# A mask that moves from TensorE into each head's bias on GpSimd, and three changed orders

## The chip, the cores and the metric

The kernel runs on one core of a Trainium2 chip. The metric is device time in microseconds (us) of one execution, as the median of the runs. PE is TensorE, DVE is VectorE, ACT is ScalarE, POOL is GpSimd, and SP is SyncE, which issues nearly all DMAs here.

## The reference, cut to what matters

Two decoder layers over 512 positions of 1024 channels, in float32. Layer 0 mixes by stick-breaking attention, layer 1 by an indexer-selected attention; each is followed by a gated MLP with a causal convolution of width 3. The second attention, for 16 heads:

```python
isc = jnp.where(causal[None], isc, NEG)          # indexer scores
_, sel = lax.top_k(isc, topk)                    # 128 keys for each query
valid = sel <= t[None, :, None]
logits = jnp.einsum('bqhd,bqkd->bqhk', qb, kg) * scale
bias = rel_bias[t5_bucket(t[None, :, None] - sel)]   # by distance, per head
logits = logits + bias
logits = jnp.where(valid[:, :, None, :], logits, NEG)
p = jax.nn.softmax(logits, axis=-1)
o = jnp.einsum('bqhk,bqkd->bqhd', p, vg)         # then w_uv, w_out
```

The kernel doesn't gather. It takes all keys up to the query's block and adds a mask of 0 or -1e30, the same for all heads, so that exactly the selected keys are left.

## The kernel before, in words

**Layout and precision.** Activations lie channel-first, 8 tiles of 128 channels by 512 positions. A product of full precision is three matmuls on a high and a low part (`mm3`, L248 to L250): high by high, low by high, high by low. A weight chunk is 128 x 1024. SP fetches it into one of six `raw` tiles (L177); `split_hi` (L208) rounds it on ACT into `whi`; `split_lo` (L216) subtracts on DVE, or on an engine it is given, into `wlo`. `whi` and `wlo` have four buffers each. All chunks follow one list, `order`; `chunk(key, 0)` returns a chunk and splits it on the spot if that hasn't happened.

**Order.** The whole kernel is under a manual schedule: each engine, and SP's queue of DMA issues, runs its instructions in the order in which the code emits them. What an instruction waits for holds up all behind it on that engine.

**Stages.** First attention (to about 245 us), its last output quarter together with the norm of the next sub-layer (`boundary`), the first feed-forward layer (to 620), `boundary`, projections and the indexer (to 770), the second attention (to 911), `boundary`, the second feed-forward layer, and the output.

**`boundary` (L376)** projects the last four chunks (`last`) in two halves of 256 positions, eight tiles each (`out_steps`, tile `pt_l`, two PSUM buffers under the tag "tr"). After each tile DVE adds it to the residual (`add_to_x`, L359) and ACT squares it. It starts by calling `chunk(k, 0)` for all four chunks.

**`bias_rows` (L167)** computes, for 16 heads and 640 distances, the bias table: two matmuls of 320 columns (L171, tile `pt_b`, tag "x", which has one buffer), each copied out by DVE (L172), and a DMA to DRAM on SP (L173). It is called before up-step 4 of the first feed-forward layer, `bias_load` before step 3. An up-step is two output tiles of 24 matmuls of 512 columns, then convolution, gate and split on ACT and DVE.

**The second attention (from L1270).** `load_bias` (L1313) fetches a head's bias as a 128 x 512 tile `th` (two buffers) whose columns run backwards. `logits(h, j)` makes query block j against its (j+1)*128 keys: three matmuls and a fourth of the identity by the mask in bf16 (L1334), which adds the mask in PSUM (tile `z`, two buffers). `softmax` scales and adds the bias (DVE, L1342) into one tile `L` per head (two buffers) and takes the row maximum (L1344); `expo` is ACT (L1349). `transposed(h, pi)` turns the block columns in three pieces on PE (L1360) and copies them out on ACT or DVE. `weighted` multiplies a pair of heads by its values (`av`), `pair_values` makes these (`pv`, tag "x"), `pair_scale` turns the reciprocal sums (`bc`, tag "x"), and `pair_hi`, `pair_lo` make the high and low parts of the pair's output `O`.

In iteration h the loop works on the transposes of head h and the logits and softmax of head h+1. Between them `fill(n)` emits n steps of other PE work, three matmuls of 512 columns each: the projections of queries 12 to 15, then the first half of the output projection (`do` chunks, tile `pt_o`), 60 steps in all. `LATE_STEPS[h]` steps go to head h, half in the middle, half at the end. Behind each step one pending event is emitted, such as splitting the next chunk or adding a finished tile.

Of the kernel before, what the change touches and what calls it, by code (L numbers as in the profile page):

```python
# [18 lines left out]
D = 1024  # L19
S = 512  # L20
# [17 lines left out]
EARLY_Q = 12  # L38
LATE_STEPS = [2, 3, 2, 3, 3, 3, 3, 3, 3, 3, 5, 5, 5, 5, 5, 8]
AHEAD = 2  # L40
# [78 lines left out]
def kernel_body(ctx, tc, xT, wst, cst, smalls, crow, ccol, relb, onehot, outT):  # L119
# [46 lines left out]

    def bias_rows():  # L167
        rsb = raws.tile([P, D], F32, name="rsb", tag="raw")[:HEADS, :640]
        for c in range(2):
            pt = ptile([P, S], "pt_b", "x")  # L170
            pe.matmul(pt[:HEADS, :320], lhsT=rel, rhs=bias["oh"][:, c * 320:(c + 1) * 320], start=True, stop=True)  # L171
            dve.tensor_copy(rsb[:, c * 320:(c + 1) * 320], pt[:HEADS, :320])  # L172
        nc.sync.dma_start(rb, rsb)  # L173

# [201 lines left out]
    def boundary(last, O, l, gate, nxt, first):  # L376


        cks = [chunk(k, 0) for k in last]
        nl, gcol, sh, sc = nxt  # L380
# [27 lines left out]
        for m in range(KT):  # L408
            t = out_tile(0, m)
            if prev is not None:  # L410
                square_add(m - 1, prev)
            prev = t
            if m == 4:
                warm(AF.Abs_reciprocal_sqrt)
# [547 lines left out]
    def ffn_layer(l, first, man):  # L962
        with ExitStack() as st:
# [54 lines left out]
            for step, i in ffn_steps():  # L1018
                if step == "up" and i < 2:
                    continue  # L1020
                if l == 0 and step == "up" and i in (3, 4):
                    (bias_load if i == 3 else bias_rows)()
                if step == "up":
                    up(i)
                elif step == "down":
                    down(i)
# [10 lines left out]
    def dsa_layer(l, first, man):  # L1037
        with ExitStack() as st:
# [233 lines left out]
            with ExitStack() as sa:  # L1272
# [9 lines left out]
                def late_steps():  # L1282

                    g, pt = late, late_pt
                    for h in range(EARLY_Q, HEADS):
                        if h > EARLY_Q:
                            pt = ptile([P, S], "pt_q", "mm")
                            g = project_steps(pt, chunk(("dq", h), 0))
                        for _ in g:
                            yield  # L1290
                        events.extend([lambda h=h, pt=pt: q_hi(h, pt), lambda h=h, pt=pt: (q_lo(h, pt), split_hi()),
                                       lambda h=h: (split_lo(), q_sum(h))])
                    events.append(lambda: q_norm(EARLY_Q, HEADS))
# [19 lines left out]
                def load_bias(h):  # L1313
                    th = ths[h] = ap.tile([P, S], F32, name="th", bufs=2)
                    ov = rb[h:h + 1, 0:1]
                    nc.sync.dma_start(th, bass.AP(tensor=ov.tensor, offset=ov.offset, ap=[[1, P], [1, S]]))

                def begin(h):
                    L = ap.tile([P, LW], F32, name="L")
# [3 lines left out]
                    heads[h] = (L, ap.tile([P, QT], F32, name="nm"), ap.tile([P, QT], F32, name="sum"), heads["rv"], {})  # L1323

                def logits(h, j):
                    qh, ql = Q[h]
                    ns = (j + 1) * P
                    qs = slice(j * P, ns)
                    ls = slice(LOFF[j], LOFF[j] + ns)
                    z = heads[h][4][j] = ptile([P, S], "z", "z")  # L1330
                    pe.matmul(z[:, :ns], lhsT=qh[:, qs], rhs=kph[:, :ns], start=True, stop=False)
                    pe.matmul(z[:, :ns], lhsT=ql[:, qs], rhs=kph[:, :ns], start=False, stop=False)
                    pe.matmul(z[:, :ns], lhsT=qh[:, qs], rhs=kpl[:, :ns], start=False, stop=False)
                    pe.matmul(z[:, :ns], lhsT=ident_b, rhs=maskb[:, ls], start=False, stop=True)  # L1334

                def softmax(h, j):
                    L, nm, sum_, rv, z = heads[h]
                    z = z.pop(j)
                    ns = (j + 1) * P
                    ls = slice(LOFF[j], LOFF[j] + ns)  # L1340
# [3 lines left out]
                    dve.tensor_reduce(nm[:, j:j + 1], L[:, ls], axis=AX.X, op=OP.max, negate=True)  # L1344

                def expo(h, j):
                    L, nm, sum_ = heads[h][:3]
                    ls = slice(LOFF[j], LOFF[j] + (j + 1) * P)
                    act.activation(L[:, ls], L[:, ls], AF.Exp, bias=nm[:, j:j + 1], accum_out=sum_[:, j:j + 1])  # L1349

                trs = {}

                def transposed(h, pi, by_act):
                    L = heads[h][0]
                    tr = ptile([P, S], "tr", "tr")
                    w = TRW[pi]
                    for i, c0 in TRP[pi]:
                        for j in range(i, QT):
                            c = c0 + (j - i) * P
                            pe.transpose(tr[:, c:c + P], L[:, LOFF[j] + i * P:LOFF[j] + (i + 1) * P], ident)  # L1360
                    if pi == 0:
# [4 lines left out]
                    else:  # L1366
                        dve.tensor_copy(t, tr[:, :w])

                vals = {}
# [61 lines left out]
                def sums(h):  # L1431

                    dve.reciprocal(heads[h][3][:, :, h % 2], heads[h][2])
                    return pair_sums(heads[h][3]) if h % 2 else None

                for h in range(HEADS):
# [165 lines left out]
```

## Time and profile before

| | us |
|---|---|
| median of 3 runs | 1310.35 (1310.23 to 1310.48) |
| the profiled execution | 1311.1 |
| its span, first to last instruction | 1309.0 |
| busy PE, DVE, ACT, POOL | 1283.9, 930.9, 591.8, 35.9 |

Busy times are unions of the spans of an engine's instructions. Matmuls overlap one another, so PE's share of 98% doesn't say that it works at its peak; a wait of PE shows best as the step from the start of one matmul to the start of the next. A bracket behind an instruction tells how long its engine sat idle before it, and what ended that.

### The profile page before, as it was taken

The numbers are of one execution on the slowest core, as the hardware profiler recorded it, in microseconds if no ns is written. First come the engines' busy times: TensorE is split into PE (matmuls) and PEld (weight loads), VectorE is DVE, ScalarE is ACT, GpSimd is POOL, SyncE is SP. The second block draws the span as 40 slices with busy tenths as digits, with TensorE's granted clock in tenths as the row PEclk, the third lists the DMA queues.
The fourth block names the chain that finished last, engine by engine and source line by source line (L and its number), as shares of the span: only waits on it lengthen the run. The fifth ranks groups of instructions, "written<-read, shape, count | busy, mean of one in ns | idle before, by whom it ended". The sixth has DMA issues, their size and how long they took to land.

```text
span 1309.0 us, 17994 instructions
## 1 busy us (share of the span) xinstructions
PE 1283.9 (98%) x6979; PEld 1069.9 (82%) x6988; DVE 930.9 (71%) x1532; ACT 591.8 (45%) x1049; POOL 35.9 (3%) x27
## 2 busy tenths in 40 slices
PE   8999999998999999999999999999999999999998
PEld 6978787896888888888987777776998888888888
DVE  5888889688677877885778877777776546546653
ACT  5576666464333433443555446565554334334430
POOL 0000000000000000000102320000000000000000
PEclk9999999999999999999999999999999999999999
DMA  9644444322576575654222301213222432433221
GB/s 374 203 129 129 145 129 133 109 69 80 210 242 192 177 243 191 194 174 153 76 65 81 97 26 54 66 58 121 79 83 73 121 97 73 121 97 97 73 89 65
DMA packets 50613, 163.23 MB, mean 125 GB/s; under 512 B 5808, under 2 KB 8624, under 8 KB 50528
## 3 DMA queue, kind: packets, MB, share of 16 engines
q1 hardware_dynamic: 50096, 161.30, 38.4%
q8 instruction: 55, 0.90, 0.3%
q10 hardware_dynamic: 432, 0.79, 0.2%
q14 instruction: 30, 0.25, 0.1%
HBM read 159.92 MB, written 2.14 MB: 124 GB/s over the span
## 4 chain that ended last, share of the span: by engine, by line
PE 91%; DVE 4%; ACT 2%; DMA 1%; issue 1%; SPq 0%; another core or an unknown queue 0%; DVEq 0%; ACTq 0%
PE pt_u L248 11%; PE pt_u L250 11%; PE pt_u L249 11%; PE pt_d L250 5%; PE pt_d L249 5%; PE pt_d L248 5%; PE pt_first L249 2%; PE pt_first L248 2%; PE pt_first L250 2%; PE pt_l L248 2%; PE pt_q L248 2%; PE pt_l L250 2%; PE pt_l L249 2%; PE pt_q L250 2%; PE pt_q L249 2%; PE pt_qk L248 2%
## 5 line engine op out<-in xcount | busy, mean ns | idle before, releaser
L208 ACT ACTIVATE whi<-raw 128x1024 fp32r<-128x1024 f32 (+1 forms) x206 | 205.1, 1002 | 122.1 <-PE pt_d L250 95.5
L248 PE MATMUL pt_u<-hhi,whi 128*128 128x512 f32 x640 | 250.1, 391 | 0.0
L249 PE MATMUL pt_u<-hhi,wlo 128*128 128x512 f32 x640 | 249.8, 390 | 0.0
L250 PE MATMUL pt_u<-hlo,whi 128*128 128x512 f32 x640 | 249.7, 390 | 0.0
L216 DVE TENSOR_TENSOR wlo<-raw,whi 128x1024 fp32r<-128x1024 f32 (+1 forms) x194 | 223.5, 1154 | 17.8 <-ACT whi L208 16.9
L973 ACT ACTIVATE y<-pt_u,sm 128x512 f32<-128x512 f32 x80 | 62.2, 777 | 200.3 <-PE pt_u L250 200.3
L248 PEld LDWEIGHTS pt_u<-hhi,whi 128*128 128x128 f32 x640 | 120.7, 189 | 26.1 <-issue 1.0
L249 PEld LDWEIGHTS pt_u<-hhi,wlo 128*128 128x128 f32 x640 | 120.7, 189 | 25.1
L250 PEld LDWEIGHTS pt_u<-hlo,whi 128*128 128x128 f32 x640 | 120.7, 189 | 25.1
L974 DVE SCALAR_TENSOR_TENSOR y<-pt_u,sm,y 128x511 f32<-128x511 f32 x80 | 59.9, 749 | 105.9 <-ACT y L973 105.9
L248 PE MATMUL pt_d<-acthi,whi 128*128 128x512 f32 x288 | 112.0, 389 | 0.0
L249 PE MATMUL pt_d<-acthi,wlo 128*128 128x512 f32 x288 | 112.0, 389 | 0.0
L250 PE MATMUL pt_d<-actlo,whi 128*128 128x512 f32 x288 | 112.0, 389 | 0.0
L257 DVE SCALAR_TENSOR_TENSOR raw<-raw,cond 128x1024 f32<-128x1024 f32 x88 | 106.5, 1216 | 1.1 <-DMA raw<-wst 1.1
L359 DVE SCALAR_TENSOR_TENSOR x<-pt_d,mod,x 128x512 f32<-128x512 f32 x48 | 36.0, 749 | 72.8 <-PE pt_d L250 72.8
L232 ACT ACTIVATE acthi<-y 128x512 fp32r<-128x512 f32 x44 | 27.8, 632 | 104.3 <-DVE y L992 104.3
L248 PE MATMUL pt_first<-hhi,whi 128*128 128x256 f32 (+1 forms) x224 | 68.6, 306 | 0.3 <-ACT whi L208 0.3
L249 PE MATMUL pt_first<-hhi,wlo 128*128 128x256 f32 (+1 forms) x224 | 67.1, 300 | 0.9 <-DVE wlo L216 0.8
L250 PE MATMUL pt_first<-hlo,whi 128*128 128x256 f32 (+1 forms) x224 | 66.9, 299 | 0.0
L249 PEld LDWEIGHTS pt_d<-acthi,wlo 128*128 128x128 f32 x288 | 54.1, 188 | 11.3
L248 PEld LDWEIGHTS pt_d<-acthi,whi 128*128 128x128 f32 x288 | 54.1, 188 | 11.2
L250 PEld LDWEIGHTS pt_d<-actlo,whi 128*128 128x128 f32 x288 | 54.1, 188 | 11.2
(253 smaller groups left out, 2662.4 us busy)
## 6 DMA issues: line engine op xcount, KB each, us to landing
raw<-wst SPq DMA_DIRECT2D x250, 512.0 KB, 3.7
raw<-wst SPq DMA_DIRECT2D x48, 384.0 KB, 3.0
th<-rb SPq DMA_DIRECT2D x16, 256.0 KB, 3.7
ada<-wst SPq DMA_DIRECT2D x4, 512.0 KB, 6.2
outT<-x SPq DMA_DIRECT2D x16, 128.0 KB, 1.7
x<-xT SPq DMA_DIRECT2D x5, 256.0 KB, 4.9
x<-xT ACTq DMA_DIRECT2D x3, 256.0 KB, 3.9
cond<-crow SPq DMA_DIRECT2D x1, 512.0 KB, 10.7
```

Source lines behind the costliest of these rows:

```text
L208: act.activation(hi[:, :n], raw[:, :n], AF.Copy)
L216: engine.tensor_sub(lo[:, :n], raw[:, :n], hi[:, :n].bitcast(F32))
L232: act.activation(hi, src, AF.Copy)
L248: pe.matmul(out, lhsT=whi, rhs=ahi, start=start, stop=False)
L249: pe.matmul(out, lhsT=wlo, rhs=ahi, start=False, stop=False)
L250: pe.matmul(out, lhsT=whi, rhs=alo, start=False, stop=stop)
L257: dve.scalar_tensor_tensor(raw, raw, 1.0, cond, op0=OP.mult, op1=OP.mult, accum_out=dst)
L359: dve.scalar_tensor_tensor(x[f][:, c], pt, mod[l][:, g * KT + f:g * KT + f + 1], x[f][:, c], op0=OP.mult, op1=OP.add)
L973: act.activation(y, pt, AF.Identity, scale=cw[2], bias=sm[:, b + S_CB + c:b + S_CB + c + 1])
L974: dve.scalar_tensor_tensor(y[:, 1:], pt[:, :S - 1], cw[1], y[:, 1:], op0=OP.mult, op1=OP.add)
```

## The change

The mask matmul goes. Each head's bias gets the mask added on GpSimd before it is used: `masked_bias(h, j)` writes `Ls[h, j]`, a tile of its own per query block (two buffers each), from the reversed bias tile and the mask. Heads 0 and 1 get theirs at the start; head h+2 gets block 0 behind the first transposes of head h, block 1 behind the second, blocks 2 and 3 behind the third. `softmax` then scales the logits and adds in place. Bias tiles are fetched two heads further ahead. Low parts of the eight chunks split in this stage go to GpSimd. The three orders: `bias_rows` does its halves before up-steps 4 and 5; `boundary` splits what is left of its last two chunks between the tiles of its first half; in the last head `pair_values` comes ahead of the filler. `LATE_STEPS` has other numbers.

```diff
-LATE_STEPS = [2, 3, 2, 3, 3, 3, 3, 3, 3, 3, 5, 5, 5, 5, 5, 8]
+LATE_STEPS = [3, 3, 3, 3, 3, 3, 3, 3, 3, 4, 5, 5, 5, 5, 4, 6]
...
+    def bias_rows(c):
+        if c == 0:
+            bias["rows"] = raws.tile([P, D], F32, name="rsb", tag="raw")[:HEADS, :640]
+        pt = ptile([P, S], "pt_b", "x")
+        pe.matmul(pt[:HEADS, :320], lhsT=rel, rhs=bias["oh"][:, c * 320:(c + 1) * 320], start=True, stop=True)
+        dve.tensor_copy(bias["rows"][:, c * 320:(c + 1) * 320], pt[:HEADS, :320])
+        if c:
+            nc.sync.dma_start(rb, bias["rows"])
...
-        cks = [chunk(k, 0) for k in last]
+        cks = [chunk(k, 0) for k in last[:2]]
+        unsplit = lambda: pos["i"] <= order.index(last[3])
...
+            if m in (0, 3) and unsplit():
+                split_hi()
+            if m in (1, 4):
+                split_lo()
+                if m == 4:
+                    while unsplit():
+                        split_hi()
+                        split_lo()
+            if m in (3, 5):
+                cks.append(chunk(last[len(cks)], 0))
...
-                if l == 0 and step == "up" and i in (3, 4):
-                    (bias_load if i == 3 else bias_rows)()
+                if l == 0 and step == "up" and 3 <= i < 6:
+                    bias_load() if i == 3 else bias_rows(i - 4)
...
-                                       lambda h=h: (split_lo(), q_sum(h))])
+                                       lambda h=h: (split_lo(engine=pool), q_sum(h))])
...
-                        events.extend([split_hi, split_lo])
+                        events.extend([split_hi, lambda: split_lo(engine=pool)])
...
+                def masked_bias(h, j):
+
+                    ns = (j + 1) * P
+                    Ls[h, j] = ap.tile([P, ns], F32, name=f"L{j}")
+                    pool.tensor_add(Ls[h, j], ths[h][:, :ns][:, ::-1], maskb[:, LOFF[j]:LOFF[j] + ns])
...
-                    pe.matmul(z[:, :ns], lhsT=qh[:, qs], rhs=kpl[:, :ns], start=False, stop=False)
-                    pe.matmul(z[:, :ns], lhsT=ident_b, rhs=maskb[:, ls], start=False, stop=True)
+                    pe.matmul(z[:, :ns], lhsT=qh[:, qs], rhs=kpl[:, :ns], start=False, stop=True)
...
-                    dve.scalar_tensor_tensor(L[:, ls], z[:, :ns], rq[:, c:c + 1], ths[h][:, :ns][:, ::-1],
-                                             op0=OP.mult, op1=OP.add)
+                    dve.scalar_tensor_tensor(L, z[:, :ns], rq[:, c:c + 1], L, op0=OP.mult, op1=OP.add)
...
+                    if h + 2 < HEADS:
+                        for j in ((0,), (1,), (2, 3))[pi]:
+                            masked_bias(h + 2, j)
...
                 load_bias(0)
                 load_bias(1)
+                for h in range(2):
+                    for j in range(QT):
+                        masked_bias(h, j)
+                    load_bias(h + 2)
...
                     if not more:
                         rvb = sums(h)
+                        pair_values(h - 1)
...
-                    if h % 2:
+                    if h % 2 and more:
                         pair_values(h - 1)
...
-                        if n + 1 < HEADS:
-                            load_bias(n + 1)
+                        if n + 3 < HEADS:
+                            load_bias(n + 3)
```

## Rows read from the trace of the kernel before

**Rows 1.** The page: its span, the ended-last chain by engine, one group of DMA issues.

```profile
span 1309.0 us, 17994 instructions
...
PE 91%; DVE 4%; ACT 2%; DMA 1%; issue 1%; SPq 0%; another core or an unknown queue 0%; DVEq 0%; ACTq 0%
...
raw<-wst SPq DMA_DIRECT2D x250, 512.0 KB, 3.7
```

**Rows 2.** Windows by stage: stretch, length, busy us per engine (instructions), clock, DMA.

```profile
770.00:914.00 144.00, 138.72 (x872) 107.55 (x880) 104.94 (x213) 83.67 (x221) 0.00 (x0) 1.00 0.23 72
```

**Rows 3.** PE's timeline: the 512-column mask matmul and its successor.

```profile
782.56 0.39 PE L1334 MATMUL z<-maskb,ident_b 128*128 128x512 bf16 x1
...
782.79 0.38 PE L1360 MATMUL tr<-cons,L 128*128 128x128 f32 x2
```

**Rows 4.** PE's timeline at the bias rows: start, us, instruction, idle before it.

```profile
318.75 0.71 PE L171 MATMUL pt_b<-oh,rel 32*16 32x320 f32 x2
324.78 1.24 PE L171 MATMUL pt_b<-oh,rel 32*16 32x320 f32 x2 [5.32 <-DVE rsb L172]
325.95 0.79 PE L248 MATMUL pt_u<-hhi,whi 128*128 128x512 f32 x1
...
330.74 0.39 PE L250 MATMUL pt_u<-hlo,whi 128*128 128x512 f32 x1
```

**Rows 5.** Windows of 4 us behind the bias rows and the last seam.

```profile
324.00:328.00 4.00, 3.22 (x7) 1.79 (x8) 2.33 (x4) 0.56 (x1) 0.00 (x0) 0.50 0.05 11
...
918.00:922.00 4.00, 4.00 (x23) 4.00 (x23) 1.09 (x3) 0.42 (x1) 0.00 (x0) 0.61 0.43 154
```

**Rows 6.** DVE's and SP's timelines at the bias rows.

```profile
324.25 0.47 DVE L172 COPY rsb<-pt_b 16x320 f32<-16x320 f32 x1
...
326.56 0.33 SPq L173 DMA_DIRECT2D rb<-rsb  x1
326.95 32.89 SPq L177 DMA_DIRECT2D raw<-wst  x15
```

**Rows 7.** DVE's and PE's timelines at the seams of 914 and 622.

```profile
913.98 2.36 DVE L216 TENSOR_TENSOR wlo<-raw,whi 128x1024 fp32r<-128x1024 f32 x2 [0.26 <-ACT whi L208]
...
917.07 0.38 PE L248 MATMUL pt_l<-ohi,whi 128*128 128x256 f32 x1 [2.55 <-DVE x L359]
...
626.05 0.36 PE L248 MATMUL pt_l<-acthi,whi 128*128 128x256 f32 x1 [1.00 <-DVE x L359]
```

**Rows 8.** POOL's timeline: copies at 650, a low part beside the top-k.

```profile
649.66 0.76 POOL L1148 COPY work<-cons 128x128 f32<-128x128 f32 x1
...
650.62 1.78 POOL L1148 COPY work<-cons 128x128 f32<-128x128 f32 x1
...
713.43 2.40 POOL L216 TENSOR_TENSOR wlo<-raw,whi 128x1024 fp32r<-128x1024 f32 x1 [5.73 <-ACT whi L208]
```

**Rows 9.** Timeline at the attention's start: head 0's first and fourth softmax step.

```profile
774.44 0.35 DVE L1342 SCALAR_TENSOR_TENSOR L<-z,cols,th 128x128 f32<-128x128 f32 x1 [1.74 <-DMA th<-rb]
...
777.47 0.75 DVE L1342 SCALAR_TENSOR_TENSOR L<-z,cols,th 128x512 f32<-128x512 f32 x1 [0.40 <-remote]
```

**Rows 10.** Timeline: a low part on DVE, PE behind it, and the last pair's scale.

```profile
833.66 1.23 DVE L216 TENSOR_TENSOR wlo<-raw,whi 128x1024 fp32r<-128x1024 f32 x1 [1.23 <-ACT whi L208]
...
835.80 0.44 PE L1331 MATMUL z<-kph,qh 128*128 128x384 f32 x1 [0.95 <-DVE L L1342]
...
908.24 0.66 PE L1406 MATMUL bc<-cons,rvb 128*128 128x128 f32 x4 [0.53 <-ACT vals L1379]
```

**Rows 11.** Timeline from head 3's third softmax step to the next iteration's transposes.

```profile
797.48 0.62 DVE L1342 SCALAR_TENSOR_TENSOR L<-z,cols,th 128x384 f32<-128x384 f32 x1 [3.31 <-PE z L1334]
...
801.66 0.33 PE L1360 MATMUL tr<-cons,L 128*128 128x128 f32 x1 [0.29 <-ACT L L1349]
...
802.29 0.40 PE L250 MATMUL pt_q<-hlo,whi 128*128 128x512 f32 x1
...
802.70 0.68 DVE L1419 TENSOR_TENSOR olo<-bs,ohi 128x512 fp32r<-128x512 f32 x1
```

More of the change, by code (lines that the diff above doesn't have):

```diff
@@ L165, in bias_load @@
         nc.sync.dma_start(bias["oh"], onehot)
[L167 to L173, printed above, removed]
+    def bias_rows(c):
[6 more added lines that the diff above has]
+            nc.sync.dma_start(rb, bias["rows"])
     def chunk_raw(key, n=D):
@@ L1316, in load_bias @@
                     nc.sync.dma_start(th, bass.AP(tensor=ov.tensor, offset=ov.offset, ap=[[1, P], [1, S]]))
+                Ls = {}
+                def masked_bias(h, j):
+                    ns = (j + 1) * P
+                    Ls[h, j] = ap.tile([P, ns], F32, name=f"L{j}")
+                    pool.tensor_add(Ls[h, j], ths[h][:, :ns][:, ::-1], maskb[:, LOFF[j]:LOFF[j] + ns])
                 def begin(h):
-                    L = ap.tile([P, LW], F32, name="L")
                     if h % 2 == 0:
@@ L1322, in begin @@
                         heads["rv"] = rv
-                    heads[h] = (L, ap.tile([P, QT], F32, name="nm"), ap.tile([P, QT], F32, name="sum"), heads["rv"], {})
+                    heads[h] = (ap.tile([P, QT], F32, name="nm"), ap.tile([P, QT], F32, name="sum"), heads["rv"], {})
                 def logits(h, j):
@@ L1328, in logits @@
                     qs = slice(j * P, ns)
-                    ls = slice(LOFF[j], LOFF[j] + ns)
-                    z = heads[h][4][j] = ptile([P, S], "z", "z")
+                    z = heads[h][3][j] = ptile([P, S], "z", "z")
                     pe.matmul(z[:, :ns], lhsT=qh[:, qs], rhs=kph[:, :ns], start=True, stop=False)
                     pe.matmul(z[:, :ns], lhsT=ql[:, qs], rhs=kph[:, :ns], start=False, stop=False)
-                    pe.matmul(z[:, :ns], lhsT=qh[:, qs], rhs=kpl[:, :ns], start=False, stop=False)
-                    pe.matmul(z[:, :ns], lhsT=ident_b, rhs=maskb[:, ls], start=False, stop=True)
+                    pe.matmul(z[:, :ns], lhsT=qh[:, qs], rhs=kpl[:, :ns], start=False, stop=True)
                 def softmax(h, j):
-                    L, nm, sum_, rv, z = heads[h]
-                    z = z.pop(j)
+                    nm, sum_, rv, z = heads[h]
+                    z, L = z.pop(j), Ls[h, j]
                     ns = (j + 1) * P
-                    ls = slice(LOFF[j], LOFF[j] + ns)
                     c = h * QT + j
-                    dve.scalar_tensor_tensor(L[:, ls], z[:, :ns], rq[:, c:c + 1], ths[h][:, :ns][:, ::-1],
-                                             op0=OP.mult, op1=OP.add)
-                    dve.tensor_reduce(nm[:, j:j + 1], L[:, ls], axis=AX.X, op=OP.max, negate=True)
+                    dve.scalar_tensor_tensor(L, z[:, :ns], rq[:, c:c + 1], L, op0=OP.mult, op1=OP.add)
+                    dve.tensor_reduce(nm[:, j:j + 1], L, axis=AX.X, op=OP.max, negate=True)
                 def expo(h, j):
-                    L, nm, sum_ = heads[h][:3]
-                    ls = slice(LOFF[j], LOFF[j] + (j + 1) * P)
-                    act.activation(L[:, ls], L[:, ls], AF.Exp, bias=nm[:, j:j + 1], accum_out=sum_[:, j:j + 1])
+                    nm, sum_ = heads[h][:2]
+                    act.activation(Ls[h, j], Ls[h, j], AF.Exp, bias=nm[:, j:j + 1], accum_out=sum_[:, j:j + 1])
                 trs = {}
                 def transposed(h, pi, by_act):
-                    L = heads[h][0]
                     tr = ptile([P, S], "tr", "tr")
@@ L1359, in transposed @@
                             c = c0 + (j - i) * P
-                            pe.transpose(tr[:, c:c + P], L[:, LOFF[j] + i * P:LOFF[j] + (i + 1) * P], ident)
+                            pe.transpose(tr[:, c:c + P], Ls[h, j][:, i * P:(i + 1) * P], ident)
                     if pi == 0:
@@ L1431, in sums @@
                 def sums(h):
-                    dve.reciprocal(heads[h][3][:, :, h % 2], heads[h][2])
-                    return pair_sums(heads[h][3]) if h % 2 else None
+                    dve.reciprocal(heads[h][2][:, :, h % 2], heads[h][1])
+                    return pair_sums(heads[h][2]) if h % 2 else None
                 for h in range(HEADS):
```

## The prediction

> **What bounds the kernel now.** I read the page first: its span line and the shares of the chain that ended last [rows 1]. 91% of the chain lies on PE, so time comes out of this kernel either as PE work removed or as PE stalls removed; a cheaper instruction on another engine counts only where PE waits for it. Then I listed the stretches by stage: the second attention runs from about 770 to 914 us, with PE busy 138.7 of 144 us, DVE 104.9, ACT 83.7 and POOL not at all [rows 2]. So PE is the bound there, DVE the next, and GpSimd is free. Last I went along PE's own timeline at each place that the diff touches, looking at the start of one matmul against the start of the next: a stall is the step beyond the usual spacing (0.23 us for 512 columns [rows 3], half of it for 256). Three stretches are worth something: the bias rows near 318, the seam near 914, and the attention itself.
>
> **Part 1, the bias rows.** `bias_rows` does both halves of the table at one point of the first feed-forward layer. Both use the one buffer of the tag "x", so the second matmul waits until DVE has copied out the first, and that copy stands in DVE's order behind all of up-step 3's evacuation: PE starts the first half at 318.75, sits for 5.32 us, starts the second at 324.78 and gets back to `pt_u` at 325.95 [rows 4]. After that idle time the granted clock is 0.50 (the 1.2 GHz level) [rows 5], and 11 matmuls take from 325.95 to 330.74, 4.79 us, where at 0.23 each they take 2.5. Price of the visit: 325.95 - 318.75 = 7.2, plus 2.3 of slow clock, 9.5 us. After the change each half is a visit of its own, an up-step (two tiles of 24 matmuls at 0.23, 11 us) apart; the first half's copy, 5.5 us after its matmul in this trace (324.25 - 318.75 [rows 6]), is long done when the second comes. Two visits at the 0.71 us of the first row cost 1.4, so the gain is 8.1 us. What it moves: the write of the table to DRAM goes out on SP when the second copy is done, and all weight fetches behind it wait; today that hold ends at 326.56 and fetching resumes at 326.95, one microsecond after PE resumes [rows 6]. After the change the write comes some 5.2 us after PE has begun up-step 5 (PE no longer stands still meanwhile), and the next weight chunk with it. By the order of the code that chunk is the second tile of up-step 6, which PE reaches 3 x 5.5 = 16.5 us after the start of step 5. Fetch issue at 5.6, 3.7 us to landing [rows 1], an ada product that DVE does first, and the low part end at about 13: some 3 us to spare. The raw-tile ring is short by two slots (the one-hot tile and the row tile live longer), which I cost at nothing behind those 3 us; if that cover goes, up to 5 us of stall come back. Bounds of the gain: 3 to 8.6 us; I take 8.1, the row's own price.
>
> **Part 2, the seams.** `boundary` splits all four last weight chunks before anything else. At the attention's end two are still whole, so DVE does 2.36 us of low parts ahead of the first residual adds; PE runs out of PSUM buffers and waits 2.55 us for the first add, until 917.07 [rows 7]. Then the clock is down again: 23 matmuls between 918 and 922 at 0.61 granted [rows 5], where 0.12 us each would make 33; 10 x 0.12 = 1.2 us. The change does these splits between the tiles. The add itself (0.48 us) cannot be hidden by two buffers, about 0.45 us stays; and the last low part, now behind the fifth tile's add, comes about 0.5 us late for the seventh tile. Gain 2.55 + 1.2 - 0.95 = 2.8. At the first layer's end PE waits 1.00 us for the same reason at 626.05 [rows 7]; I keep half, 0.5. The seam at 249 loses half a microsecond and gets no price. Sum 3.3, bounds 1.5 to 5.
>
> **Part 3, the second attention.** Removed: 64 mask matmuls. The one of 512 columns takes its place from 782.56 to the next start at 782.79, 0.23 us [rows 3]; a head has 1280 columns, so 0.23 x 1280/512 = 0.575, times 16 = 9.2 us of PE. Added: per head four GpSimd adds over 1280 columns. The nearest row is GpSimd's two-input subtract, 2.40 us for 1024 columns [rows 8]: 3.0 us a head, and 3.4 with an allowance of mine of 0.1 us for each instruction's start. An upper price is the 128-column copy, 0.76 us [rows 8], 5.9 ns a column, 7.6 us a head. I take 3.4, because the subtract is the same kind of instruction and the copies ran beside DVE instructions that fetch two SBUF tensors. With the eight moved low parts (8 x 2.4 / 16 = 1.2) GpSimd has 4.6 us of work in a head of about 8.2, and each add is issued at least half a head before its softmax: hidden, except at the start. There the bias tile lands at 774.4 and DVE starts at once, while the 512-column step runs at 777.47 [rows 9]. With 3.4 us of GpSimd work ahead of the fourth softmax it starts near 777.9: 0.4 later, and PE, which stands behind this chain, gets nothing of the 0.7 us of masks inside it. Minus 1.1 (bounds 0.3 and 4).
>
> What else changes in the stage. A low part on DVE stands ahead of a softmax: DVE takes 1.23 us for it from 833.66, and PE waits 0.95 us for a logits buffer at 835.80 [rows 10]; the same recurs near 888 at half the size. On GpSimd these go: plus 1.5. The value projection moved ahead of the last filler saves PE's 0.53 us wait for the bank at 908.24 [rows 10]: plus 0.5. The chain from the third logits (797.48) over two softmax steps, a PSUM copy and the exponential to the last transpose (801.66) takes 4.2 us [rows 11] and doesn't get shorter, while PE's work beside it loses about 0.4 us of masks. One filler step (0.68 us) more in heads 0 and 2 removes what PE waits there; heads 4, 6 and 8 begin to wait by about 0.3 each: nothing in sum. With the new step table the last quarter of the first output tile falls in the middle of head 9, right behind the transposes, where today it falls one or two steps later; it needs the fourth pair's low part, which DVE starts at 802.70 in a head of this kind, 0.68 us, while PE's third filler matmul comes at 802.29 [rows 11]: minus 1.0. DVE delayed by GpSimd at the pair's low part and broadcast copy (16 instructions, two-input or copy): minus 1.0 by the stretched copy of 1.78 us against 0.76 [rows 8], about 1 us each at half the cases, of which an eighth reaches PE. SP: each bias load now waits for GpSimd rather than DVE; the weight fetches behind it have a whole chunk (8 filler steps, more than one head) to spare. Sum 9.2 - 1.1 + 1.5 + 0.5 - 1.0 - 1.0 = 8.1, bounds 3 to 11.
>
> GpSimd's two-input instruction costs twice DVE's 1.23 us [rows 8, 10], and all twelve of its kind beside the top-k took the same 2.40 us. The Trainium skill (GPSIMD Engine Reference, 4.1 Engine selection) speaks against the change: elementwise arithmetic belongs on VectorE. Its other rule (SBUF - State Buffer, Who interferes with whom) is that GpSimd reads and a DVE instruction with two SBUF inputs lock each other out whole; by that rule the softmax steps, with one input in PSUM, would stay free, and the 1.78 us copy agrees with it.
>
> **The sum.** 8.1 + 3.3 + 8.1 = 19.5. The profiled execution took 1311.1 us, its span 1309.0 [rows 1]; it would become 1291.6. The median of the runs, 1310.35, is 0.75 below it and becomes 1290.85: I predict 1290.8.
>
> **Rivals.** (a) The attention is held by DVE rather than PE once the masks are gone: PE's cover is thinner than the 4.2 us chain in every head, and the stage gives its lower bound 3. For: DVE at 73% of the stage; against: in most heads the weighted sums (2.3 us) lie beside the chain. 1310.35 - 8.1 - 3.3 - 3 = 1296.0. (b) The bias write holds up the weight fetches and PE waits for up-step 6: 5 us come back, 1295.8. For: no transfer at all ran during today's hold; against: the 3 us to spare. (c) GpSimd costs the copy's 7.6 us a head: 8.8 with the low parts, against 8.2. The stage then takes 16 x 8.8 = 141 us, as today, and starts 4 us late: 1310.35 - 11.4 + 4 = 1303. (d) Slower: GpSimd and DVE block each other in every head, as the copy was stretched by 1.78/0.76 = 2.3. Then a head needs 2.3 x 4.6 = 10.6 us of GpSimd, 170 us for the stage, 30 more than today's 140: 1310.35 - 11.4 + 30 = 1329. It decides from about 9.5 us a head, (140 + 11.4)/16. Against it: the twelve low parts beside the top-k kept 2.40 us, and of DVE's instructions in this stage few have two SBUF inputs. (e) The change does not do what it says: the split bias halves still meet in the buffer, the masks' place goes to waits: within 2.6 us of before.
>
> **How the numbers follow.** My case 0.70 (1286 to 1294), (a) 0.11, (b) 0.08, (c) 0.04, (d) 0.04, (e) 0.03. The range 1285.6 to 1298 holds my case, (a) and (b) with their spread; its low end is the three upper bounds, 8.6 + 5 + 11 = 24.6 below 1310.35. A measurement of this kernel can tell about 0.2%, 2.6 us, from no change: faster 0.93, same 0.03, slower 0.04.
>
> **What would show it.** Right: no PE wait between two `pt_b` matmuls and a clock of 1.00 there; PE's step at the seam under 1 us; no matmul that reads `maskb`; GpSimd adds of about 3.4 us a head that no `L` on DVE waits for after head 1; the stage shorter by 7 to 9 us. Wrong: `pt_u` waiting for a low part near 345 us (b), DVE waiting for POOL in each head (c, d), or PE waits before the first transpose of most heads (a).

## The result and the profile after

| | before | after |
|---|---|---|
| median of 4 runs each, us | 1310.29 (1310.06 to 1310.48) | 1294.13 (1293.74 to 1295.02) |
| ratio, 95% interval | | 0.9878 (0.9861 to 0.9895) |
| span of the profiled execution, us | 1309.0 | 1292.2 |

16.2 us went, where 19.5 were forecast, and 1294.13 lies inside the range. I cut both spans at four instructions of PE's timeline: the first `pt_l` of the first, second and third seam, and the attention's first `z`. The last column is the forecast for what changes in the stretch.

| stretch, us | before | after | difference | forecast |
|---|---|---|---|---|
| start to the first seam | 245.85 | 245.71 | -0.1 | 0 |
| first feed-forward layer (bias rows) | 376.16 | 368.30 | -7.9 | -8.1 |
| seam at 622 to the attention | 148.91 | 149.13 | +0.2 | -0.5 |
| second attention | 140.21 | 134.35 | -5.9 | -8.1 |
| last seam and the rest | 397.87 | 394.71 | -3.2 | -2.8 |

So the miss is in the attention; no other stretch is off by as much as one microsecond. The page of after, its span, busy PE and POOL, and the chain that ended last by engine, answers to [rows 1]:

```profile
span 1292.2 us, 18031 instructions
...
PE 1272.0 (98%) x6924; PEld 1064.4 (82%) x6924; DVE 926.1 (72%) x1524; ACT 591.0 (46%) x1049; POOL 106.7 (8%) x99
...
PE 92%; DVE 3%; ACT 2%; DMA 1%; issue 1%; SPq 0%; POOL 0%; DVEq 0%; ACTq 0%; POOLq 0%
```

POOL's busy time has tripled, from 35.9 to 106.7 us, and yet its share of the chain is 0%: the added work is nearly all beside PE's. The bias rows, by the tile `pt_b` in after (instruction and count: shortest, median and longest ns, first and last start), and the two windows of [rows 5]:

```profile
L171 PE MATMUL pt_b<-oh,rel x4: 427/432/439, 318.6 to 330.6; 32*16 32x320 f32 x4
...
L172 DVE COPY rsb<-pt_b x2: 472/472/472, 324.1 to 335.9; 16x320 f32<-16x320 f32 x2
...
324.00:328.00 4.00, 4.00 (x19) 3.31 (x18) 3.85 (x6) 2.17 (x3) 0.00 (x0) 1.00 0.50 157
...
918.00:922.00 4.00, 4.00 (x32) 3.86 (x32) 4.00 (x9) 2.95 (x8) 0.00 (x0) 1.00 0.34 108
```

The first half is copied at 324.1 and the second half runs at 330 without a wait; the 5.32 us of [rows 4] are gone, and the clock stays at 1.00 where it was 0.50. Behind the last seam it is 1.00 too, with 32 matmuls where there were 23.

What PE waits for in the second attention (who, on what, us in sum, times, longest), first before, then after:

```profile
PE z L1331 <- DVE L L1342: 2.8, 3, 1.4
PE tr L1360 <- ACT L L1349: 1.3, 3, 0.5
PE bc L1406 <- ACT vals L1379: 0.5, 1, 0.5
```

```profile
PE z L1349 <- DVE L L1358: 2.9, 2, 2.2
PE pt_o L251 <- DVE olo L1435: 1.7, 1, 1.7
PE tr L1373 <- ACT L L1363: 0.8, 1, 0.8
PE ssq L1091 <- ACT vals L1395: 0.7, 1, 0.7
PE pt_o L249 <- ACT ohi L1431: 0.6, 1, 0.6
```

With the masks gone PE works less and waits more: 6.7 us against 4.6. It waits most at two places. In head 9 the 0.57 and 1.68 us are new. At the start, where [rows 9] had DVE begin as soon as the bias landed, GpSimd's eight adds now come first, and PE's wait for a logits buffer, 1.40 us before, is 2.25 (GpSimd's row, then PE's):

```profile
766.85 6.10 POOL L1336 TENSOR_TENSOR L<-th,maskb 128x128 f32<-128x128 f32 x8 [8.73 <-DMA th<-rb]
```

```profile
767.72 0.44 PE L1349 MATMUL z<-kph,qh 128*128 128x384 f32 x1 [2.25 <-DVE L L1358]
```

At both places there is something that no sum had: the windows of after at the start, and those of another run of the same kernel (`after_again` below) at the start and in head 9:

```profile
768.00:772.00 4.00, 4.00 (x14) 3.24 (x14) 3.17 (x6) 1.81 (x6) 4.00 (x6) 0.61 0.22 48
```

```profile
768.00:772.00 4.00, 4.00 (x14) 3.21 (x13) 2.86 (x5) 1.39 (x5) 4.00 (x6) 0.57 0.22 66
...
844.00:848.00 4.00, 4.00 (x21) 3.62 (x20) 3.13 (x8) 1.27 (x3) 0.68 (x1) 0.68 0.00 0
```

The granted clock fell from its 2.4 GHz level to the 1.2 GHz one for a part of these windows, in one execution once, in the other twice, with the same code and, in head 9, the same waits ahead (0.57 and 1.68 in both). From the weighted sum of heads 6 and 7 to that of heads 8 and 9 (`av`, start to start) the first took 18.34 us, the other 19.93: the fall in head 9 costs about 1.6 us. The one at the start costs about 0.9: from the first `z` to the first `av` after takes 21.79 us, and `pair_pool` (below), with the same adds and steps there and a clock of 1.00, takes 20.87. Before had none inside the attention.

And DVE itself is slower at some places. DVE's timeline in after, and beside it POOL's (start, us, instruction):

```profile
840.54 2.24 DVE L1435 TENSOR_TENSOR olo<-bs,ohi 128x512 fp32r<-128x512 f32 x1
...
859.38 2.48 DVE L1435 TENSOR_TENSOR olo<-bs,ohi 128x512 fp32r<-128x512 f32 x1
```

```profile
839.87 2.36 POOL L217 TENSOR_TENSOR wlo<-raw,whi 128x1024 fp32r<-128x1024 f32 x1 [1.42 <-ACT cols L1093]
...
858.90 2.40 POOL L217 TENSOR_TENSOR wlo<-raw,whi 128x1024 fp32r<-128x1024 f32 x1 [1.42 <-ACT whi L209]
```

The pair's low part `olo` is a subtraction of two SBUF tiles of 512 columns; it takes 0.69 us by its median in the same trace, and before it never took more than 0.69. Twice it begins some half a microsecond to 0.7 us behind a GpSimd subtraction, and twice it ends just behind that one: at 842.78 and 861.86, where POOL ends at 842.23 and 861.30. GpSimd's own instruction keeps its 2.4 us. The one that begins first holds the other: `olo` at 794.85 keeps its 0.69, and the mask add of 256 columns that begins beside it at 795.19 takes 0.89 us where the median is 0.68.

### The profile page after: what moved, and what is told of

The parts are those of the page before. It is cut to its first block, busy times and chain, and to the rows that moved or that the text cites. A ratio compares the mean times of both kernels' runs of the same rounds, so it can differ in the third digit from the quotient of the medians.

```text
span 1292.2 us, 18031 instructions
## 1 busy us (share of the span) xinstructions
PE 1272.0 (98%) x6924; PEld 1064.4 (82%) x6924; DVE 926.1 (72%) x1524; ACT 591.0 (46%) x1049; POOL 106.7 (8%) x99
## 4 chain that ended last, share of the span: by engine, by line
PE 92%; DVE 3%; ACT 2%; DMA 1%; issue 1%; SPq 0%; POOL 0%; DVEq 0%; ACTq 0%; POOLq 0%
PE pt_u L249 11%; PE pt_u L250 11%; PE pt_u L251 11%; PE pt_d L250 5%; PE pt_d L251 5%; PE pt_d L249 5%; PE pt_first L250 2%; PE pt_first L249 2%; PE pt_first L251 2%; PE pt_q L249 2%; PE pt_q L251 2%; PE pt_q L250 2%; PE pt_l L250 2%; PE pt_l L249 2%; PE pt_l L251 2%; PE pt_qk L249 2%
## 5 line engine op out<-in xcount | busy, mean ns | idle before, releaser
L217 DVE TENSOR_TENSOR wlo<-raw,whi 128x1024 fp32r<-128x1024 f32 (+1 forms) x186 | 214.0, 1151 | 12.5 <-ACT whi L209 11.5
L250 PEld LDWEIGHTS pt_d<-acthi,wlo 128*128 128x128 f32 x288 | 54.1, 188 | 11.2
```

Of the source, the lines that this page charges most:

```text
L217: engine.tensor_sub(lo[:, :n], raw[:, :n], hi[:, :n].bitcast(F32))
L250: pe.matmul(out, lhsT=wlo, rhs=ahi, start=False, stop=False)
```

## The experiments

Each row's gain is against the kernel before on the same chip, in whose runs its median lay between 1310.7 and 1311.4; the attention's length is of the profiled execution, cut as above.

| kernel | median, us | gain | ratio, 95% interval | attention, us |
|---|---|---|---|---|
| `bias_only` | 1302.98 | 8.1 | 0.9939 (0.9924 to 0.9954) | 140.35 |
| `seam_only` | 1308.97 | 2.1 | 0.9985 (0.9975 to 0.9994) | 140.32 |
| `mask_only` | 1307.73 | 3.4 | 0.9977 (0.9968 to 0.9987) | 137.10 |
| `mask_lo_pool` | 1306.00 | 5.4 | 0.9958 (0.9943 to 0.9973) | 136.45 |
| `lo_on_dve` | 1299.84 | 11.2 | 0.9917 (0.9901 to 0.9934) | 141.01 |
| `old_steps` | 1296.25 | 15.1 | 0.9883 (0.9866 to 0.9899) | 137.49 |
| `after_again` | 1294.52 | 16.6 | 0.9872 (0.9857 to 0.9887) | 136.08 |
| `step_later` | 1295.24 | 16.1 | 0.9880 (0.9866 to 0.9895) | 134.84 |
| `pair_pool_old` | 1296.61 | 14.5 | 0.9893 (0.9876 to 0.9909) | 135.66 |
| `pair_pool` | 1291.59 | 19.8 | 0.9848 (0.9834 to 0.9863) | 130.29 |
| `head0_dve` | 1293.56 | 17.1 | 0.9866 (0.9850 to 0.9883) | 134.11 |
| `head0_pe` | 1290.42 | 20.7 | 0.9840 (0.9825 to 0.9854) | 130.07 |

### The parts one by one

**The bias rows alone**, in the kernel before:

```diff
-                if l == 0 and step == "up" and i in (3, 4):
-                    (bias_load if i == 3 else bias_rows)()
+                if l == 0 and step == "up" and 3 <= i < 6:
+                    bias_load() if i == 3 else bias_rows(i - 4)
```

> The kernel before with one part of the change: the two bias halves ahead of up-steps 4 and 5. If the price read from PE's timeline holds, 8.1 us are gained, 1302.2, with no idle time between the two pt_b matmuls and a granted clock of 1.00 behind them. If the table's write holds up the weight fetches on SP, up to 5 us of PE waits come back near up-step 6, 1307.

8.1 us by the medians and 7.9 in the stage; the clock at 324 to 328 is 1.00. The part's price was the row's own price.

**The seams alone**, in the kernel before:

```diff
-        cks = [chunk(k, 0) for k in last]
+        cks = [chunk(k, 0) for k in last[:2]]
...
+            if m in (0, 3) and unsplit():
+                split_hi()
+            if m in (1, 4):
+                split_lo()
```

> The kernel before with one part of the change: boundary splits the last two chunks between its tiles. Both the forecast (2.8 at the attention's end, 0.5 at the first layer's end) and the landmarks of the changed kernel (3.3 at the one, a loss of 0.2 at the other) say about 3.2 us in sum, 1307.1; they differ in the step at the first layer's end: PE's wait of 1.00 us there halves, or is replaced by waits for the two low parts of the same length. If the splits between the tiles delay PE as much as they did ahead of them, no gain.

2.1 by the medians (0.8 to 3.3 by the interval), less than the 3.2 expected. The last seam gave 2.9 us. At 622 nothing came; PE's timeline of this kernel there:

```profile
626.69 0.36 PE L248 MATMUL pt_l<-acthi,whi 128*128 128x256 f32 x1 [0.31 <-DVE x L359]
...
633.45 0.39 PE L249 MATMUL pt_l<-acthi,wlo 128*128 128x256 f32 x1 [0.49 <-DVE wlo L216]
```

Of the 1.00 us of [rows 7] 0.31 is left, and a new wait of 0.49 stands 7 us behind it: the last low part, moved behind the adds, comes late for its tile. That late low part was in the forecast for the seam at 914, and forgotten for the one at 622, where the order is the same.

**The mask alone**, in the kernel before: `masked_bias`, one `L` per block and the earlier bias loads, with the low parts left on DVE and the old step table:

```diff
-                    pe.matmul(z[:, :ns], lhsT=ident_b, rhs=maskb[:, ls], start=False, stop=True)
...
+                    pool.tensor_add(Ls[h, j], ths[h][:, :ns][:, ::-1], maskb[:, LOFF[j]:LOFF[j] + ns])
```

> The kernel before with the mask's move alone: GpSimd adds, a tile for each block, bias tiles fetched earlier; low parts on DVE, old step table, old order of the last head. The PE theory says that the 9.2 us of mask matmuls come back less 1.1 at the start and about 1 us where heads with three filler steps lose their cover, 7 us, 1303.3. The rival, that DVE's chain holds the stage, says that half or more of the masks' time turns into waits of PE before the first transposes of each head: 3 to 4.5 us, 1306 to 1307.

The 9.2 us of mask matmuls gave 3.1 in the stage, not 7. So rival (a) was right for this edit by itself. What PE waits for in the attention of this kernel:

```profile
PE z L1337 <- DVE L L1346: 6.5, 7, 2.1
PE tr L1361 <- ACT L L1351: 1.9, 3, 0.6
PE ssq L1079 <- ACT vals L1383: 0.7, 1, 0.7
PE bc L1410 <- ACT vals L1383: 0.5, 1, 0.5
```

The waits for a logits buffer grow from 2.8 to 6.5 us. One of them, DVE first and PE behind it:

```profile
831.16 1.34 DVE L216 TENSOR_TENSOR wlo<-raw,whi 128x1024 fp32r<-128x1024 f32 x1 [1.23 <-ACT whi L208]
832.42 0.68 DVE L1416 TENSOR_TENSOR bs<-av,bs 128x512 f32<-128x512 f32 x1
833.02 0.34 DVE L1346 SCALAR_TENSOR_TENSOR L<-z,cols,L 128x128 f32<-128x128 f32 x1
```

```profile
833.41 0.45 PE L1337 MATMUL z<-kph,qh 128*128 128x384 f32 x1 [1.54 <-DVE L L1346]
```

DVE idles 1.23 us for ACT, then does the low part and the pair's sum, and only then the softmax that PE waits for. Before, with the masks on PE, the waits for `z` summed to 2.8.

**The low parts.** One kernel puts them on GpSimd with the mask (`mask_lo_pool` is `mask_only` with this edit), the other is after with them back on DVE:

```diff
-                                       lambda h=h: (split_lo(engine=pool), q_sum(h))])
+                                       lambda h=h: (split_lo(), q_sum(h))])
...
-                        events.extend([split_hi, lambda: split_lo(engine=pool)])
+                        events.extend([split_hi, split_lo])
```

> The mask's move alone plus the eight low parts on GpSimd; old step table, old last head, old seams and bias rows. Theory now: without the masks a low part on DVE, with its wait for ACT's high part, stands ahead of a softmax that PE has no more work to cover, and moving these is worth about 4 us on top of the mask's 3.3: 1303.5. Rival, the step table and the last head's order made the other 5 us between the changed kernel and its variant with low parts on DVE: then 1306.5 to 1307.5, no better than the mask's move alone.

> The changed kernel with the eight low parts of this stage back on DVE. If GpSimd's low part and the pair's low part on DVE shut each other out, the two stretched pair parts (2.24 and 2.48 us) fall to 0.69, and PE's wait of 2.3 us at the last quarter of the first output tile falls to about 1; but the two waits behind a low part on DVE return (1.5 us): within 1 us of the changed kernel. If the stretched parts have another cause (the order of the steps alone), they stay, and the kernel is 1.5 us slower than the changed one.

In the old order the move is worth 2.0 us by the gains (5.4 against 3.4; 4 were expected), in the new one 5.4 (16.6 against 11.2; at most 1.5 were expected). Both are net: the move also brings the subtractions on GpSimd that hold `olo`, for which the forecast had 1.5 less 1.0. In the old order the two profiles differ by only 0.6 us in the attention, and the trace of `mask_lo_pool` shows why, DVE first, then PE:

```profile
831.68 2.28 DVE L1423 TENSOR_TENSOR olo<-bs,ohi 128x512 fp32r<-128x512 f32 x1
```

```profile
837.88 0.39 PE L1337 MATMUL z<-kph,qh 128*128 128x256 f32 x1 [1.76 <-DVE L L1346]
...
838.44 4.07 PE L1396 MATMUL av<-pT,vals 128*64 128x512 f32 x16
```

`olo` is held, the softmax steps behind it come late, PE waits 1.76 us, and the clock falls behind that wait (0.81 at 836 to 840, 0.76 at 840 to 844): the 16 matmuls of the weighted sum take 4.07 us, where they take 2.38 in after.

In the new order, with the low parts on DVE, PE waits 10.9 us in the attention, against 6.8 in `after_again`. Its longest waits in `lo_on_dve`:

```profile
PE z L1349 <- DVE L L1358: 5.0, 4, 2.1
PE pt_o L249 <- ACT ohi L1431: 2.6, 1, 2.6
PE tr L1373 <- ACT L L1363: 2.0, 3, 0.8
...
PE pt_o L251 <- DVE olo L1435: 0.6, 1, 0.6
```

and the clock falls twice, at 800 to 808 and at 844 to 852. The same trace says what stretched `olo` in after: with no subtraction on GpSimd beside it, it never takes more than 0.69 us.

```profile
L1435 DVE TENSOR_TENSOR olo<-bs,ohi x8: 679/682/693, 795.5 to 905.8; 128x512 fp32r<-128x512 f32 x8
```

```profile
L1435 DVE TENSOR_TENSOR olo<-bs,ohi x8: 682/692/2479, 794.9 to 899.1; 128x512 fp32r<-128x512 f32 x8
```

(first `lo_on_dve`, then after). No mask add begins ahead of an `olo` that it overlaps in `lo_on_dve`, so whether one could stretch it isn't shown.

### Head 9 and the step table

The forecast took 1.0 us off for the step of the output projection that now falls into head 9. Two kernels change `LATE_STEPS` of after alone: the old table, and one that moves a step out of heads 8 and 9.

```diff
-LATE_STEPS = [3, 3, 3, 3, 3, 3, 3, 3, 3, 4, 5, 5, 5, 5, 4, 6]
+LATE_STEPS = [2, 3, 2, 3, 3, 3, 3, 3, 3, 3, 5, 5, 5, 5, 5, 8]
```

```diff
-LATE_STEPS = [3, 3, 3, 3, 3, 3, 3, 3, 3, 4, 5, 5, 5, 5, 4, 6]
+LATE_STEPS = [3, 3, 3, 3, 3, 3, 3, 3, 2, 3, 5, 5, 5, 6, 5, 6]
```

> The changed kernel with the step table of before. The last quarter of the first output tile is then emitted one or two steps later in head 9, so PE's wait of 2.3 us for the fourth pair's high and low part should go; heads 0 and 2 have one filler step less and wait about 0.3 us each, and the last heads have more steps. Theory of the wrong step: about 1.5 us faster than the changed kernel. Rival, the table matters as a whole by the cover it gives heads 0 to 9: slower by 1 us or more.

> The changed kernel with only heads 8 to 13 of the step table changed (2, 3, 5, 5, 5, 6), so that the last quarter of the first output tile comes at the end of head 9. The wait of 2.3 us there goes: 2 us faster than the changed kernel, if nothing else moves; the two low parts of GpSimd that stretch the pair's low part on DVE to 2.2 and 2.5 us may now fall beside other instructions.

Neither gained: 15.1 and 16.1 us against 16.6, so that `old_steps` came out as its rival said. In both the wait of head 9 is gone, and PE waits for a logits buffer instead: 5.1 us in four waits in `old_steps` and 5.2 in five in `step_later`, against 2.9 in two in after. In `old_steps` the clock also falls twice, at 832 to 836 and 848 to 852 (0.61 and 0.60). So the place of the step can't be all of it. The theory that remained: the held `olo` stands in DVE's order ahead of the next softmax, and PE meets it at the one or at the other.

> The changed kernel unchanged, on the same chip as the others of this call, so that they are compared with it directly: 0.986 to 0.990 of the kernel before. In its first profile the clock fell behind the wait at the stage's start; whether it does so here too is open, and 1.2 us hang on that.

After itself, run beside them: 1294.52, 0.4 above the first time, and with the second fall of the clock shown above.

### The lock

If `olo` is what holds, it can go where the instruction that blocks it is:

```diff
-                    dve.tensor_sub(O[-1][1], pair["bs"], O[-1][0].bitcast(F32))
+                    pool.tensor_sub(O[-1][1], pair["bs"], O[-1][0].bitcast(F32))
```

`pair_pool_old` is after with this line, `pair_pool` has the table of `step_later` as well.

> As the one before, and the pair's low part on GpSimd too, where it follows GpSimd's own instructions in order and DVE has no instruction left in this stage that reads two SBUF tensors. If the lock between the two engines costs PE anything beyond the step in head 9, this is another 1 us faster than step_later; if the stretched pair parts were only seen by PE in head 9, the same within 0.5 us, since DVE loses 8 x 0.69 us of work that isn't on the path.

> The changed kernel with one line else: the pair's low part on GpSimd, the step table as it is. If the lock between the two engines costs PE by holding all of DVE's queue (softmax steps behind the stretched pair part), the stage gains about 2 us although the low part itself now comes later in head 9, behind GpSimd's own low part: PE's wait there grows to 3 us. If the lock costs only through head 9, the kernel is 0.5 to 1 us slower than the changed one.

With the later step it is 3.7 us faster than `step_later`, more than the 1 us expected; with after's own table it is 2 us slower than after. On GpSimd `olo` takes 1.29 us and stands in line behind the weight's low part; with after's table the matmul that needs it comes at once and waits 2.79 us (head 9, `pair_pool_old`), and the clock falls there:

```profile
843.60 0.57 PE L251 MATMUL pt_o<-olo,whi 128*128 128x512 f32 x1 [2.79 <-POOL olo L1435]
```

```profile
844.00:848.00 4.00, 4.00 (x16) 3.48 (x15) 2.37 (x5) 0.54 (x2) 0.67 (x1) 0.59 0.00 0
```

So the two edits belong together: the step table decides whether a late `olo` costs anything, the engine decides who else is late. The profiled execution of `pair_pool` had no fall of the clock at all, though, so its gain mixes two causes. The next two kernels part them. Both take head 0's mask back to PE at the start, where DVE and PE waited for eight GpSimd adds:

```diff
+                    if h == 0:
+                        pe.matmul(z[:, :ns], lhsT=ident_b, rhs=maskb[:, LOFF[j]:LOFF[j] + ns], start=False, stop=True)
...
+                        if h:
+                            masked_bias(h, j)
```

DVE then reads head 0's bias from the fetched tile, and the bias tiles of heads 2 and 3 are fetched behind head 0's last softmax step. `head0_pe` is `pair_pool` with that, `head0_dve` the same with `olo` back on DVE.

> As pair_pool, with head 0's mask still added by PE and its bias read by DVE straight from the fetched tile, as in the kernel before, so that nothing waits for GpSimd at the start. The start was priced at 1.1 us: PE's wait for the third logits falls from 2.1 to about 1.4 us, PE does 0.6 us of mask matmuls more: 0.3 to 0.8 us faster than pair_pool. If the start of the stage is set by the bias tiles' landing alone, no difference beyond 0.3 us.

> head0_pe with the pair's low part (olo, 512 columns) back on VectorE; the step table and head 0's mask by TensorE stay. It closes the square of two edits: step_later (VectorE, mask of head 0 on GpSimd, 1295.2), pair_pool (GpSimd, GpSimd, 1291.6), head0_pe (GpSimd, TensorE, 1290.4). Theory: of the 3.6 us between step_later and pair_pool about 2.7 are VectorE's low part held up beside GpSimd's instructions, and 0.9 the clock that fell at the start; without that fall the low part alone is left: 1293.1 (1292.4 to 1293.8), olo with a median of 0.69 and at least two of over 2 us, PE waits for z of 3 to 5 us in sum, no window below 0.98 at 768 to 776. Rival: the clock made the difference and the held low part is covered: at most 1 us above head0_pe, 1290.4 to 1291.4.

Against `pair_pool`, `head0_pe` gains 0.9 us, but its attention is only 0.2 shorter, with a clock of 1.00 in both profiled executions: PE's wait at the start is 1.41 us instead of 2.08, and PE does 0.58 us of masks more. The rest of the 0.9 goes with the lower mean clock of `pair_pool`'s other runs (0.998 and 0.999); its one run at 1.000 took 1290.03.

The mean granted clock was 1.00 in all four runs of `head0_pe` and of `head0_dve`, and the runs lie close: 1290.03 to 1290.69 and 1293.31 to 1294.00. So `olo` on DVE instead of GpSimd, with the clock out of it, costs 3.1 us by the medians, and 3.6 by the gains and by the spans of the two profiled executions (1292.2 and 1288.6); in the attention alone it is 4.0, and the last seam gives 0.6 back, where PE waits 0.33 us for `olo` from GpSimd. The time and the signs that were expected of `head0_dve` came. PE's waits in the attention, first `head0_dve`, then `head0_pe`:

```profile
PE z L1349 <- DVE L L1361: 4.7, 5, 1.7
PE tr L1376 <- ACT L L1366: 1.2, 2, 0.6
PE ssq L1091 <- ACT vals L1398: 0.7, 1, 0.7
```

```profile
PE z L1349 <- DVE L L1361: 1.7, 2, 1.4
PE tr L1376 <- ACT L L1366: 1.2, 2, 0.6
...
PE ssq L1091 <- ACT vals L1398: 0.4, 1, 0.4
```

3.0 us of it lie in the waits for `z` alone. The edit also takes 8 x 0.69 us of work out of DVE's order, but that work alone isn't what PE waits for: `olo` is held in three of its eight places in `head0_dve` (840.00, 858.12 and 875.47, 2.23 to 2.48 us), waits for `z` of 1.36, 0.68 and 0.66 us that `head0_pe` doesn't have stand behind these three, and none stands behind the five of 0.68 to 0.69. One of the waits, from `olo` to PE:

```profile
840.00 2.26 DVE L1438 TENSOR_TENSOR olo<-bs,ohi 128x512 fp32r<-128x512 f32 x1
...
844.10 1.27 DVE L1416 COPY rvb<-rv 128x512 f32<-128x512 f32 x1
845.29 0.74 DVE L1361 SCALAR_TENSOR_TENSOR L<-z,cols,L 128x512 f32<-128x512 f32 x1
```

```profile
846.09 0.39 PE L1349 MATMUL z<-kph,qh 128*128 128x256 f32 x1 [1.36 <-DVE L L1361]
```

`olo` loses 1.6 us to the weight's low part, the broadcast copy 0.8 (0.43 us where nothing holds it) to a mask add, and the softmax behind them is up to 2.4 us late, of which PE waits 1.36. The step from `step_later` to `head0_dve`, 1.7 us by the medians (1.0 by the gains), is head 0's mask and the falls of the clock. `head0_pe` is the fastest of all: 20.7 us below the kernel before and about 4 below after.

## Why the prediction was right, and where not

**Part 1, right.** 8.1 forecast, 8.1 measured alone. The hold of the weight fetches behind the table's write came as told and cost nothing: by SP's timeline (where [rows 6] had 326.56 and 326.95) the write goes out 5.4 us after PE has begun up-step 5 (331.00), the next fetch behind it, and PE waits for no weight from there to the seam. Rival (b) fell.

```profile
336.37 0.33 SPq L174 DMA_DIRECT2D rb<-rsb  x1
336.75 2.87 SPq L178 DMA_DIRECT2D raw<-wst  x6
```

**Part 2, right in sum.** 3.3 forecast, 3.2 - 0.2 = 3.0 in the profiles. The last seam gave more than its 2.8, since only 0.22 + 0.49 us of waits stay where 0.95 were allowed, and the clock stays up; the seam at 622 gave nothing, where I kept 0.5. The step that failed there is "I keep half": the late low part, charged at the other seam, was left out. That 3.0 stands so near to 3.3 is luck: the two went against each other.

**Part 3, the direction right, the size not.** 8.1 forecast, 5.9 and 4.1 measured in two executions; the sign "shorter by 7 to 9 us" didn't come. By its terms:

- *The price of the adds* was right: eight adds took 6.10 us at the start, 3.05 a head against 3.4. So rivals (c) and (d) had no ground, and no softmax waits for POOL after the start. By blocks an add takes 0.43, 0.68, 0.93 and 1.17 us by its median for 128 to 512 columns; the subtraction of [rows 8] was the right neighbour, the copy wasn't.
- *The 9.2 us of masks* are PE work removed, but alone they give 3.1 to 3.4. The forecast argued that the weighted sums beside the chain are cover enough, against (a); `mask_only` shows they aren't while low parts stand in DVE's order. This is the largest miss of the sum. With the low parts and `olo` both out of that order, in `pair_pool`, the attention is 9.9 us shorter than before.
- *The low parts, plus 1.5*, come with the lock in one edit, plus 0.5 in sum: 2.0 by the gains in the old order (0.6 in the stage, with a fall of the clock in it), 5.4 in the new. In the new order 1.5 was too small: I counted two waits that the trace of before showed, and not those that the masks had covered. The misses went against each other, so that mask and low parts together gave 5.4 alone (3.8 in the stage), where 9.2 - 1.1 + 1.5 - 1.0 = 8.6 was the sum for them.
- *The lock, minus 1.0*, is of the terms charged against the gain the one that was mis-sized most: 3.1 us by `head0_dve` against `head0_pe`. I took the copy's stretch of 1 us, half the cases, and an eighth to PE. The stretch itself was right: in `head0_dve` 7 of the 16 instructions are longer, by 8.0 us in sum (4 of 16 and 4.2 us in after), where half the cases make 8. The eighth was wrong: 2.7 of the 8.0 us, a third, reach PE as waits for `z`, since the held instruction stands ahead of the softmax that frees a logits buffer.
- *Head 9, minus 1.0*: 0.57 + 1.68 = 2.25 in after. 1.55 of it is the lock again (2.24 against 0.69): the place was right, the reason only half.
- *The start, minus 1.1*, is near: PE waits 0.85 more there. `pair_pool`, which has the adds, is 0.2 us longer in the attention than `head0_pe`, which does head 0's masks (0.58 us) on PE, so the adds take back those masks and 0.2 more, about 0.8. In after the fall of the clock comes on top.
- *The last head, plus 0.5*, came: PE's wait for `bc` is gone.
- *The clock inside the attention* was in no term. It fell once or twice in after, at about 0.9 us at the start and 1.6 in head 9. That TensorE slows behind a stall was in the prediction at the bias rows and the last seam; that the change makes new stalls of its own, and pays for those too, was not.

One sum of the range is off, and nothing hangs on it: 24.6 below 1310.35 is 1285.75, not 1285.6.

The Trainium skill's rule (SBUF - State Buffer, Who interferes with whom) says that a DVE instruction with two SBUF inputs and a GpSimd instruction that reads SBUF lock each other out for a whole instruction. The traces agree on the subtraction (0.69 to 2.24 and 2.48), and on what stays free: the softmax's scale-and-add, with one input in PSUM, has a longest of 0.75 us before and after, though 34 of its 64 steps in after begin beside a running GpSimd instruction. The list of instructions that can take the pair, in the same section of the Trainium skill, holds copies, and the broadcast copy agrees with that (0.43 to 1.27). The Trainium skill's rule against elementwise work on GpSimd (GPSIMD Engine Reference, 4.1 Engine selection) would have cost here: GpSimd's subtraction is indeed twice as long (2.4 against 1.23 us), and moving it there still won 2.0 to 5.4 us; PE waits for DVE's order, and in after's attention it meets GpSimd's pace only at the start.

## What to carry to other kernels

Work taken off the bound engine is worth what that engine doesn't then wait for: before pricing it, list what stands in the next engine's order ahead of the instruction that frees a buffer, and take that out in the same change. When a long two-input instruction goes to GpSimd, look through DVE's order for those with two SBUF inputs or plain copies beside it, and price each at what is left of the GpSimd instruction that begins ahead of it, and then by what stands behind it; moving the victim to GpSimd too helps only if its consumer is late enough. And a stall that a change makes on TensorE can have a second price in granted clock.

## What the runs showed of the hardware

- A DVE subtraction of 512 columns from two SBUF tiles went from 0.69 to 2.24 and 2.48 us (after) and to 2.23, 2.26 and 2.48 (`head0_dve`) beside a GpSimd subtraction of 1024 columns that had begun 0.5 to 0.7 us earlier and kept its 2.4; beside GpSimd's mask adds (at most 1.4 us) the broadcast copy went from 0.43 to between 0.76 and 1.33 us in the same two runs, and not in every case.
- The same code with the same stall of PE ahead had the clock fall in one execution and not in another, and the runs of one kernel follow it: `pair_pool` ran from 1290.03 (mean clock 1.000) to 1292.59 (0.998), `mask_only` from 1307.27 (0.996) to 1309.64 (0.993), while `head0_pe`, with 1.000 in every run, spread by 0.7 us. What decides in a given execution stays open.
- The stretch to the first seam, which no kernel changes, differed by up to 2.2 us between executions (245.1 to 247.4); a difference of one microsecond between two profiles is to be read by stage.
